# An unused 32-byte buffer beside the raw weights of a hybrid attention block: the ring of weight tiles moves down by 32 bytes in each partition

## The chip, the cores and the metric

The kernel runs on one core of one Trainium2 chip. The metric is device time in microseconds (us) of one execution. Three runs of the kernel before gave 836.05, 835.23 and 834.75 us, a median of 835.23 us.

## The reference

One layer of a decoder block on 512 tokens of width 1024. A projection of the normalised input feeds two token mixers, a chunked gated linear attention (GLA, 4 heads) and a sparse attention with a compressed, a selected and a window branch (NSA, 8 heads). Their gated sum goes through an output matrix and a normalisation, then a SwiGLU network of width 2816 follows. Cut to its frame:

```python
proj = rms_norm(x, norm_mix_pre) @ w_in
o_gla = gla_mixer(g_q, g_k, g_v, g_r, g_a, ...)
o_nsa = nsa_mixer(n_q, n_kc, n_vc, n_ks, n_vs, n_kw, n_vw, n_gate, ...)
mixed = sigmoid(merge_gla) * (o_gla @ w_proj_gla) + sigmoid(merge_nsa) * (o_nsa @ w_proj_nsa)
x = x + rms_norm(mixed @ w_out, norm_mix_post)
h = rms_norm(x, norm_ffn_pre)
f = (silu(h @ w_ffn_gate) * (h @ w_ffn_up)) @ w_ffn_down
x = x + rms_norm(f, norm_ffn_post)
```

All inputs and the output are float32.

## The kernel before

**Split products.** Every large product is made of three matmuls in the type fp32r. A weight tile is split into a high part and a low part (the rest), an activation tile likewise, and lines 243, 248 and 249 (function `three`) add high weight by high activation, high weight by low activation, and low weight by high activation. In the profile the first name behind the arrow is the moving operand, the second the stationary one that a weight load (PEld) brings into the array ahead of its matmul. Activations move and weights are stationary, except in line 569, the first projection (`w_tok`), where the weight tile moves (440 columns) and the activation is stationary.

**Stages.** From the start to about 66 us runs the first projection, with 440 columns a matmul. Up to 200 us follow products in a Strassen-like form (line 352 makes their sums), 256 columns a matmul, with some plain products of 512 columns between them. From 200 to 460 us most products move 512 columns: GLA's end, the compressed branch, from about 275 to 415 us the attention itself with transposes of the probabilities (line 1139), then the second part of `w_proj` (moving tiles `bh`, `bl`) and the first three products of `w_out`. From 460 to 705 us the matmuls move 256 columns again: the rest of `w_out` by halves, then the gate and up matrices of the SwiGLU network in the Strassen-like form. From 705 to 765 us the first part of `w_down` moves 512 columns, and the rest of `w_down`, again in that form, 256.

**Weights.** A raw weight tile (`wraw`, 128 by 1024, 4 KB in each partition, three buffers) is loaded by SyncE. ScalarE casts it to its high part `whi` (line 78 and others), VectorE subtracts to get the low part `wlo` (line 85 and others), or a DMA of GpSimd's queue adds the raw weights onto a negated high part (lines 82 and 1446). Two pairs of `whi` and `wlo` form the ring. Other weights stand in tiles of the left side: `d_two`, `c_two`, `w_uu`, `w_g3h`, `w_g3l`, `feq`, `eks`, `ekw`.

**Where tiles lie.** Class `Ring` holds two pools on the right side of the memory: `raws` for `wraw`, and below it the pool `ring`, which is closed and opened anew twice. `open(16)` puts a gap of 64 bytes above the four ring tiles, `open(0)` does not. So the ring lies at one of two places: from the opening at the kernel's start, and again from the fourth product of `w_out` on, it is at "place A"; from the nineteenth tile of the first stream of weights (about 210 us) to the third product of `w_out` (about 460 us) at "place B", 64 bytes lower. Below the ring, still on the right side, lie the attention's probabilities (`p`, `p0`, `mx`, `z`) and some merge gates (`tb`).

Addresses below are bytes within a partition, as the built program has them. In the kernel before, `wraw` begins at 217056 (32 mod 64, 96 mod 128); the ring at 200672 in place A (96 mod 128) and 200608 in place B (32 mod 128). The moving activations of lines 243 to 249 begin at 32 mod 128 nearly everywhere (`hT_hi` at 17824); the weights on the left side at 96 mod 128 (`d_two` at 161504).

**Order.** Each engine's list of instructions is laid down as the program is written, with `issue_after` and priorities as hints to the scheduler; semaphores tie the engines together. A function `restart` makes the next 256-column product issue its second matmul as two of 128 columns.

Of the kernel before, what the change touches and what calls it, by code (L numbers as in the profile page):

```python
# [8 lines left out]
F32 = mybir.dt.float32  # L9
# [27 lines left out]
class Stream:  # L37


    def __init__(self, tc, pool, ahead):  # L40
        self.tc, self.nc, self.pool, self.ahead, self.after = tc, tc.nc, pool, ahead, None
        self.src, self.done, self.pos, self.made = [], {}, 0, 0
        self.on_dma, self.place, self.limit, self.by_half, self.raws = set(), {}, None, set(), {}
        self.reset = None
# [59 lines left out]
class Ring:  # L104


    def __init__(self, ctx, tc):
        self.tc, self.pool, self.turn = tc, None, {}
        self.raws = ctx.enter_context(tc.tile_pool(name="raws", bufs=1, side="right"))
        ctx.callback(self.close)  # L110

    def close(self):
        if self.pool is not None:
            self.pool[1].__exit__(None, None, None)
        self.pool = None
# [1942 lines left out]
```

## Time and profile before

The profile shows one execution whose span, from the first to the last instruction, is 833.8 us. The page gives no total of that execution beside its span; the runs' median is 835.23 us, 1.4 us more than the span.

| engine | busy us | share of the span |
|---|---|---|
| PE (matmul) | 823.1 | 99% |
| PEld (weight load, beside PE) | 749.7 | 90% |
| DVE (VectorE) | 633.1 | 76% |
| ACT (ScalarE) | 526.2 | 63% |
| POOL (GpSimd) | 147.2 | 18% |

The matmul row is a union of overlapping spans: each matmul's span reaches past the start of the next, so a busy share of 99% says that the array was never without a matmul, not that it ran at its peak. The pace is read from the distance between starts (the timeline view) or from the count of matmuls in a stretch that is wholly busy. The granted TensorE clock is 1.00 in all stretches but the last.

### The profile page before, as it was taken

How to read it: one execution, taken by the hardware profiler on the slowest of the kernel's cores; microseconds unless marked ns; L12 is line 12 of the kernel's file. 1: busy time of each engine (PE TensorE's matmuls, PEld its weight loads, DVE VectorE, ACT ScalarE, POOL GpSimd, SP SyncE). 2: the span in 40 equal slices, each digit the busy share in tenths (PEclk: the TensorE clock that was granted, in tenths of full speed). 3: DMA queues.
4: the chain of work that ended last, by engine and by line, in shares of the span. 5: the costliest groups of instructions: out<-in, count | busy, mean ns of one | idle time of the engine just before them, and what ended most of it. 6: DMA issues, size and time to landing. Idle time of an engine off the chain costs nothing.

```text
span 833.8 us, 14626 instructions
## 1 busy us (share of the span) xinstructions
PE 823.1 (99%) x5553; PEld 749.7 (90%) x5553; DVE 633.1 (76%) x1198; ACT 526.2 (63%) x973; POOL 147.2 (18%) x176
## 2 busy tenths in 40 slices
PE   9999999999999999999999999999999999999996
PEld 8998899998788787888888999999999999889996
DVE  7765897883377888777666488998888778839985
ACT  6557767763454889887645587766665657535542
POOL 0101022230030000100000365111211110001354
PEclk9999999999999999999999999999999999999998
DMA  8333465762252454454228758789878883325333
GB/s 295 98 110 102 120 121 129 168 145 84 76 182 51 105 127 101 102 127 106 73 76 280 227 153 228 141 209 236 187 187 200 201 182 86 91 77 178 89 103 101
DMA packets 41239, 117.85 MB, mean 141 GB/s; under 512 B 4716, under 2 KB 7036, under 8 KB 41040
## 3 DMA queue, kind: packets, MB, share of 16 engines
q1 hardware_dynamic: 27952, 82.49, 31.9%
q0 software_dynamic: 12496, 33.88, 22.0%
q8 instruction: 43, 0.70, 0.3%
q10 hardware_dynamic: 720, 0.54, 0.2%
q14 instruction: 28, 0.23, 0.1%
HBM read 102.21 MB, written 4.19 MB: 128 GB/s over the span
## 4 chain that ended last, share of the span: by engine, by line
PE 88%; DVE 5%; ACT 4%; POOL 2%; issue 1%; POOLq 0%; DVEq 0%; ACTq 0%
PE ps_mm L243 13%; PE ps_mm L249 13%; PE ps_mm L248 13%; PE ps_sc L243 5%; PE ps_sc L249 5%; PE ps_sc L248 4%; PE ps_acc L248 3%; PE ps_acc L249 3%; PE ps_acc L243 3%; PE ps_tp L249 2%; PE ps_tp L243 2%; PE ps_tp L248 2%; PE ps_tp L569 2%; PE ps_sc L569 2%; PE ps_tp L1139 2%
## 5 line engine op out<-in xcount | busy, mean ns | idle before, releaser
L78 ACT CAST whi<-wraw 128x1024 fp32r<-128x1024 f32 (+2 forms) x62 | 60.2, 973 | 64.9 <-PE ps_mm L248 22.7
L243 PE MATMUL ps_mm<-hT_hi,whi 128*128 128x512 f32 (+1 forms) x260 | 100.1, 385 | 0.2 <-ACT whi L78 0.2
L249 PE MATMUL ps_mm<-hT_hi,wlo 128*128 128x512 f32 (+1 forms) x260 | 97.1, 374 | 0.0
L248 PE MATMUL ps_mm<-hT_lo,whi 128*128 128x512 f32 (+1 forms) x259 | 96.7, 374 | 0.0
L85 DVE TENSOR_TENSOR wlo<-wraw,whi 128x1024 fp32r<-128x1024 f32 (+2 forms) x47 | 51.4, 1096 | 27.0 <-ACT whi L78 26.9
L243 PEld LDWEIGHTS ps_mm<-hT_hi,whi 128*128 128x128 f32 x260 | 48.9, 188 | 10.2 <-ACT whi L78 0.9
L249 PEld LDWEIGHTS ps_mm<-hT_hi,wlo 128*128 128x128 f32 x260 | 48.8, 188 | 9.3 <-DVE wlo L85 0.3
L248 PEld LDWEIGHTS ps_mm<-hT_lo,whi 128*128 128x128 f32 x259 | 48.7, 188 | 7.5
L1462 ACT CAST d_two<-s 128x1024 fp32r<-128x1024 f32 x26 | 27.0, 1044 | 30.5 <-PE ps_mm L249 15.0
L274 DVE TENSOR_TENSOR pl<-ps_tp,ph 128x512 fp32r<-128x512 f32 (+1 forms) x64 | 31.2, 490 | 13.2 <-ACT ph L273 12.5
L1469 DVE TENSOR_TENSOR d_two<-s,d_two 128x1024 fp32r<-128x1024 f32 x25 | 30.6, 1223 | 11.2 <-ACT d_two L1462 10.9
L82 POOL DMA_DIRECT2D wlo<-wraw x15 | 12.8, 852 | 147.3 <-ACT wlo L81 71.3
L1101 ACT ACTIVATE p<-p,mx 128x512 f32<-128x512 f32 (+3 forms) x64 | 35.7, 559 | 4.6 <-DVE mx L1099 4.2
L1099 DVE CUSTOM_DVE_ANT_0 p<-ps_sc,causal 128x512 f32<-128x512 f32 (+3 forms) x64 | 30.0, 488 | 9.5 <-PE ps_sc L1093 8.6
L273 ACT CAST ph<-ps_tp 128x512 fp32r<-128x512 f32 (+1 forms) x64 | 26.6, 417 | 4.4 <-PE ps_tp L1139 3.4
L1838 POOL TENSOR_TENSOR y<-y,us 128x256 f32<-128x256 f32 x12 | 16.0, 1361 | 72.1 <-DVE us L1835 72.1
L1139 PE MATMUL ps_tp<-ident,p 128*128 128x128 f32 x160 | 27.7, 272 | 0.0
L1139 PEld LDWEIGHTS ps_tp<-ident,p 128*128 128x128 f32 x160 | 20.8, 140 | 7.2 <-ACT pc L1023 0.4
L1446 POOL DMA_DIRECT2D wlo<-in_w_gate x13 | 11.5, 887 | 76.8 <-ACT wlo L1444 76.7
L1462 ACT CAST c_two<-s 128x1024 fp32r<-128x1024 f32 x12 | 12.5, 1044 | 18.7 <-PE ps_acc L249 9.5
L243 PE MATMUL ps_mm<-hT_hi,d_two 128*128 128x256 f32 x80 | 22.3, 279 | 0.0
L249 PE MATMUL ps_mm<-hT_hi,d_two 128*128 128x256 f32 x80 | 22.3, 279 | 0.0
(841 smaller groups left out, 3214.6 us busy)
## 6 DMA issues: line engine op xcount, KB each, us to landing
wraw<-in_w_t SPq DMA_DIRECT2D x36, 512.0 KB, 3.9
wraw<-in_w_gate SPq DMA_DIRECT2D x21, 512.0 KB, 4.5
rw<-in_w_up SPq DMA_DIRECT2D x19, 512.0 KB, 8.3
wlo<-wraw POOLq DMA_DIRECT2D x15, 512.0 KB, 4.5
wlo<-in_w_gate POOLq DMA_DIRECT2D x13, 512.0 KB, 8.6
w_uu<-in_w_up POOLq DMA_DIRECT2D x19, 256.0 KB, 8.7
wraw<-in_w_tok SPq DMA_DIRECT2D x11, 440.0 KB, 3.4
wraw<-in_w_proj SPq DMA_DIRECT2D x8, 512.0 KB, 3.6
```

The source lines that it names most:

```text
L78: self.cast = self.nc.scalar.copy(hi[:, :cols], raw[:, :cols])
L85: self.nc.vector.tensor_tensor(out=lo[:, :cols], in0=raw[:, :cols], in1=hi[:, :cols].bitcast(F32), op=OP.subtract)
L243: pe.matmul(o, wh, xh, start=start, stop=False, skip_group_check=True)
L248: pe.matmul(o[:, c], wh, xl[:, c], start=False, stop=False, skip_group_check=True)
L249: return pe.matmul(o, wl, xh, start=False, stop=stop, skip_group_check=True)
L274: dve.tensor_tensor(out=lo, in0=src, in1=hi.bitcast(F32), op=OP.subtract)
L569: pe.matmul(o, x[:, k, t], y[:, w], start=(k == 0 and m == 0), stop=(k == KD - 1 and m == 2))
L1099: dve.tensor_tensor_reduce(out=o, in0=s, in1=causal[:, S - 128 * (i + 1):S], scale=-1.0, scalar=-NEG, op0=OP.add, op1=OP.min, accum_out=mx ...
L1101: act.activation(out=o, in_=o, func=AF.Exp, scale=-1.0, bias=mx[:, i:i + 1], accum_out=z[:, i:i + 1])
L1139: pe.transpose(tp[:, i * 128:(i + 1) * 128], p[:, OFF[i] + k * 128:OFF[i] + (k + 1) * 128] if i else p0, ident)
L1462: act.copy(hi, t)
L1469: dve.tensor_tensor(out=lo, in0=t, in1=hi.bitcast(F32), op=OP.subtract)
```

## The change

One tile of 128 partitions by 8 float32 (32 bytes in each partition) is asked for in the pool `raws`, before any raw weight tile. Nothing writes or reads it.

```diff
@@ -108,6 +108,7 @@
         self.tc, self.pool, self.turn = tc, None, {}
         self.raws = ctx.enter_context(tc.tile_pool(name="raws", bufs=1, side="right"))
         ctx.callback(self.close)
+        self.raws.tile([128, 8], F32, name="line")
 
     def close(self):
         if self.pool is not None:
```

No engine's list of instructions changes: all five hold the same rows in the same order with the same waits, apart from line numbers and buffer numbers. What changes is addresses. The words for the change are that raw weights and ring begin at 0 instead of 32 mod 64. In the built program the new room lies at the low end of `raws`, between it and the ring: the three `wraw` buffers keep their addresses (32 mod 64), and SyncE's instructions are the same byte for byte. All that lies below moves down by 32 bytes:

| tiles | before | after |
|---|---|---|
| `wraw` | 217056 (96 mod 128) | 217056 (96 mod 128) |
| ring, place A | 200672 (96 mod 128) | 200640 (64 mod 128) |
| ring, place B | 200608 (32 mod 128) | 200576 (0 mod 128) |
| `p`, three buffers | 32 mod 128 | 0 mod 128 |
| `p0`, `mx`, `z`, seven `tb` | 32 bytes lower each | |

Every tile on the left side stays.

## Prediction

> **What bounds the kernel now.** I read the page's busy shares and chain first.
>
> ```profile
> span 833.8 us, 14626 instructions
> PE 823.1 (99%) x5553; PEld 749.7 (90%) x5553; DVE 633.1 (76%) x1198; ACT 526.2 (63%) x973; POOL 147.2 (18%) x176
> PE 88%; DVE 5%; ACT 4%; POOL 2%; issue 1%; POOLq 0%; DVEq 0%; ACTq 0%
> ```
>
> TensorE carries 88% of the chain of waits. A change that moves no instruction can only act through how long instructions take, and only TensorE's pace reaches the end. So the second view is a table by stage of stretches in which TensorE is wholly busy (columns: stretch, its length, then busy time and count of PE, PEld, DVE, ACT and POOL, the granted clock, the DMAs):
>
> ```profile
> 446.00:459.00 13.00, 13.00 (x59) 10.74 (x59) 5.69 (x6) 7.66 (x10) 1.28 (x1) 1.00 0.96 355
> 542.00:554.00 12.00, 12.00 (x104) 12.00 (x104) 11.72 (x21) 6.58 (x10) 1.71 (x2) 1.00 0.76 209
> 570.00:700.00 130.00, 130.00 (x1149) 130.00 (x1149) 104.63 (x185) 80.11 (x124) 21.34 (x25) 1.00 0.80 185
> 720.00:740.00 20.00, 20.00 (x87) 16.14 (x86) 9.73 (x14) 7.19 (x11) 0.00 (x0) 1.00 0.30 81
> ```
>
> The clock is full in all four, and nobody waits. The third view is the timeline, for the distance between starts; first and last row of each stretch:
>
> ```profile
> 456.04 0.39 PE L249 MATMUL ps_mm<-hT_hi,wlo 128*128 128x512 f32 x1
> ...
> 459.44 0.39 PE L249 MATMUL ps_mm<-hT_hi,wlo 128*128 128x512 f32 x1
> ```
> ```profile
> 744.96 0.39 PE L243 MATMUL ps_acc<-hT_hi,whi 128*128 128x512 f32 x1
> ...
> 749.16 0.39 PE L243 MATMUL ps_tp<-hT_hi,whi 128*128 128x512 f32 x1
> ```
> ```profile
> 599.75 0.28 PE L243 MATMUL ps_sc<-x4h,w_g3h 128*128 128x256 f32 x1
> ...
> 603.49 0.28 PE L243 MATMUL ps_tp<-hT_hi,whi 128*128 128x256 f32 x1
> ```
> ```profile
> 546.89 0.28 PE L243 MATMUL ps_mm<-x,d_two 128*128 128x256 f32 x1
> ...
> 549.36 0.28 PE L249 MATMUL ps_tp<-hT_hi,d_two 128*128 128x256 f32 x1
> ```
>
> The first holds 15 steps in 3.40 us, 226.7 ns a matmul; the second 18 in 4.20 us, 233.3 ns. Both move 512 columns of the same `hT` against ring tiles, in the same form; what differs is where the ring lies: place B at 32 mod 128, place A at 96 mod 128, with the moving tile at 32 in both. The third holds 33 steps in 3.74 us, 113.3 ns for 256 columns; the fourth 21 in 2.47 us, 117.6 ns, with weights (96) and moving tiles (32) at the same places as in the third. So this core has two paces for each width, 3 to 4% apart. For 512 columns the offset between weights and moving tile goes with the pace (64 bytes apart is slow); for 256 columns, 64 bytes apart can be fast, and something in the history decides, since 542 to 554 us ran slowly and 570 to 700 us (1149 in 130 us) at the fast pace throughout. A stream of moving data and a stream of weights are read at the same time, and their relative phase matters: that is how I read it. It is argued from pace alone. One more case, moving tiles partly at 96, ring at 32:
>
> ```profile
> 420.95 0.39 PE L243 MATMUL ps_sc<-bh,whi 128*128 128x512 f32 x1
> ...
> 423.74 0.40 PE L243 MATMUL ps_sc<-bh,whi 128*128 128x512 f32 x1
> ```
>
> 12 steps in 2.79 us, 232.5 ns: in 8 of the 12 the moving tile (`bl`, and half of `bh`) stands 64 bytes off, and it is the slow pace again.
>
> No row of this trace has fp32r weights at 0 or 64 mod 128: that is what the change brings.
>
> **The change part by part.** Counts of matmuls are of the program; the ring is stationary in 336 of 512 columns at place A (14 products of 24), 744 of 512 at place B, and 1236 of 256 at place A; it moves in 288 of 440.
>
> *Ring at place B, 512 columns.* Of the 744, the attention's 360 and the 96 with `bh` already run between the paces or slowly (the row above, and in the attention the mean span is 392 where the fast stretch has 389 and the slow one 396):
>
> ```profile
> L248 PE MATMUL ps_mm<-hT_lo,whi 128*128 128x512 f32 x74 | 29.0, 392 | 0.0
> ```
> ```profile
> L243 PE MATMUL ps_mm<-hT_hi,whi 128*128 128x512 f32 x20 | 7.8, 389 | 0.0
> ```
> ```profile
> L243 PE MATMUL ps_sc<-hT_hi,whi 128*128 128x512 f32 x8 | 3.2, 396 | 0.0
> ```
>
> The other 288 are fast. Between nothing and the whole distance of 6.6 ns, that is 0 to +1.9 us; if all 744 were fast now, +4.9 us is the outer bound. The new place lies 32 bytes off the moving tile, midway between the two that are measured, so I take the middle, +3.3 ns: +1.0 us.
>
> *Ring at place A, 512 columns.* These 336 are slow now and can only keep that or gain: −2.2 us to 0, the middle −1.1 us.
>
> *Ring at place A, 256 columns.* Some of the 1236 stand in slow stretches; I take three quarters, 930, as fast now (an estimate from 570 to 700 us being fast and 542 to 554 us slow). 0 to +4.3 ns each; the middle 2.15 ns gives +2.0 us, the outer bound with all 1236 is +5.3 us.
>
> *The neighbours.* 2131 more matmuls of 256 columns take their weights from the left side, still at 96. Today all weights in the SwiGLU stage lie alike; afterwards ring tiles at 64 and others at 96 alternate, and each change of place shifts the phase. A slow stretch outlives the product that began it (the fourth timeline is slow on `d_two` alone). Bounds: the 145 us from 560 to 705 us, all fast now, slow down by 117.6/113.3, +5.5 us; or slow stretches elsewhere are cured, −1.5 us for the 40 us around 542 to 554 us. Loss has more room than gain here; I take a fifth of the loss, +1.1 us.
>
> *Ring as the moving operand, 440 columns.* A tile has two halves of 440 columns, 1760 bytes apart: one begins at 96 mod 128, the other at 64. The row that tells what 0 mod 64 does to a moving operand is therefore in the trace:
>
> ```profile
> 50.12 0.36 PE L569 MATMUL ps_tp<-whi,hu_hi 128*128 128x440 f32 x1
> 50.32 0.36 PE L569 MATMUL ps_tp<-whi,hu_lo 128*128 128x440 f32 x1
> 50.52 0.36 PE L569 MATMUL ps_tp<-wlo,hu_hi 128*128 128x440 f32 x1
> 50.72 0.36 PE L569 MATMUL ps_tp<-whi,hu_hi 128*128 128x440 f32 x1
> 50.92 0.36 PE L569 MATMUL ps_tp<-whi,hu_lo 128*128 128x440 f32 x1
> 51.12 0.36 PE L569 MATMUL ps_tp<-wlo,hu_hi 128*128 128x440 f32 x1
> 51.32 0.36 PE L569 MATMUL ps_sc<-whi,hu_hi 128*128 128x440 f32 x1
> ```
>
> Three from either half take 0.60 us. The halves now begin at 64 and 32. Zero, with a bound of 288 times 3% of 200 ns, ±1.7 us, by the two paces of the other widths.
>
> *Casts, subtractions and DMAs.* The cast onto the ring and the subtraction take what the same forms take on tiles elsewhere:
>
> ```profile
> L78 ACT CAST whi<-wraw 128x1024 fp32r<-128x1024 f32 x43 | 44.9, 1049 | 48.5 <-PE ps_mm L248 19.3 <-issue 10.3 <-PE ps_tp L248 5.4
> L1462 ACT CAST d_two<-s 128x1024 fp32r<-128x1024 f32 x26 | 27.0, 1044 | 30.5 <-PE ps_mm L249 15.0 <-PE ps_acc L249 13.9 <-DVE s L1478 1.4
> L85 DVE TENSOR_TENSOR wlo<-wraw,whi 128x1024 fp32r<-128x1024 f32 x28 | 34.1, 1222 | 18.9 <-ACT whi L78 18.8
> L1469 DVE TENSOR_TENSOR d_two<-s,d_two 128x1024 fp32r<-128x1024 f32 x25 | 30.6, 1223 | 11.2 <-ACT d_two L1462 10.9
> ```
>
> A few ns of a microsecond, and 99% of matmul time covers both engines; without that cover, 5 ns on each of some 110 such instructions would be 0.6 us. The raw weights do not move, so SyncE's loads cost nothing new, whatever the words for the change say. The DMAs that add onto `wlo` land as here:
>
> ```profile
> wlo<-wraw POOLq DMA_DIRECT2D x15, 512.0 KB, 4.5
> L249 PEld LDWEIGHTS ps_mm<-hT_hi,wlo 128*128 128x128 f32 x260 | 48.8, 188 | 9.3 <-DVE wlo L85 0.3
> ```
>
> The weight loads that use `wlo` name no DMA as what they waited for, so these too are covered; 10% on the landing would be 0.5 us inside slack.
>
> Sum: +1.0 − 1.1 + 2.0 + 1.1 = +3.0 us on the span of 833.8, 836.8; the runs lie about 1.4 us above it, **838.2 us**.
>
> [...]
>
> **The rivals.**
>
> *Nothing below 64 bytes matters* (chance 0.24). The pace would follow which 64-byte half of a 128-byte stretch a tile begins in, and 96 to 64, or 32 to 0, stay in their halves. For it: the 440-column halves at 96 and 64 are equal. Against: nothing measured, since 64 bytes is the smallest distance by which weights differ in this trace. Time 835.2, ±1 us. [...]
>
> *The ring lands in the good phase* (0.23). The 336 slow ones become fast, −2.2 us, and the slow 40 us are cured, −1.5: 831.5 us. For it: the two measured places each suit one width and fail the other, so neither is best for both. Against: most of the time is at the fast pace already.
>
> *Loads that begin on a 64-byte line are shorter* (0.06). 512 bytes from 32 mod 64 touch nine lines of 64 bytes, from 0 eight. If the 113.3 ns were set by the load and fell to the pace of the transposes, about 0.11 us each (four of them end 0.60 us after the first began, each spanning 272 ns),
>
> ```profile
> 321.98 0.60 PE L1139 MATMUL ps_tp<-ident,p 128*128 128x128 f32 x4
> L1139 PE MATMUL ps_tp<-ident,p 128*128 128x128 f32 x160 | 27.7, 272 | 0.0
> ```
>
> that is 3%: some −4 us on the 1236, −5 on the 744 and as much on the 336 with their way from 233.3: about 821 us. Against: a fast 512-column matmul has room for two loads and still takes twice 113.3.
> [...]
>
> *The phase slips for good* (0.10; the slow side at its full price). All ring products at the slow pace, +4.9 and +5.3, and half of the 2131 neighbours times 4.3 ns, +4.6, less 2.2: +12.6, 847.8 us. It decides from the point where a ring product leaves the next `d_two` product in the slow pace. For it: slow stretches last. Against: `restart` stands at the stages' beginnings.
>
> **How the numbers follow.** The moderate loss has 0.37, its own range 837 to 842. With 0.10 for the slip, slower holds 0.47; the first rival is same, 0.24; faster 0.23 + 0.06 = 0.29. Beyond 0.2%, 1.7 us, a measurement of this kernel tells a change from none. Range: 829 to 845, which leaves out the shorter loads and the full slip.
>
> **What would show it.** In the new profile: the 512-column span of 389 near 446 to 459 us and 396 near 720 to 740 us, the 276 of 256 columns between 570 and 700 us and the count of 1149 there. Middle values, or both 276 and 281 mixed by product, bear me out; all four unchanged is the first rival; 389 at 720 us with 276 kept is the second; under 276 the third. I am wrong if the time moves while these rows stand, since then DMAs or ScalarE carry it.

## The result and the profile after

The changed kernel took 840.62 us (median of four runs, 840.41 to 841.55) against 835.63 us for the kernel before beside it (834.75 to 836.05). The ratio is 1.0065, with a 95% interval of 1.0053 to 1.0077: slower by 5.0 us, on the side and within the range of the forecast, which had a loss of 3.0 us.

The first view is the page of the kernel after: the span, the engines' busy times, and the shares of the chain of waits.

```profile
span 838.7 us, 14626 instructions
...
PE 828.8 (99%) x5553; PEld 754.8 (90%) x5553; DVE 633.5 (76%) x1198; ACT 526.1 (63%) x973; POOL 146.2 (17%) x176
...
PE 93%; ACT 3%; DVE 2%; issue 1%; POOL 0%; POOLq 0%; ACTq 0%
```

The span grew by 4.9 us. TensorE's busy time grew by 5.7 us, VectorE's by 0.4, and ScalarE's and GpSimd's shrank a little. So the time is in TensorE's pace, as a change without a moved instruction suggests. The second view is the table by stage that the prediction used, of the kernel after (stretch, its length, busy time and count of PE, PEld, DVE, ACT, POOL, granted clock, DMA share, GB/s):

```profile
446.00:459.00 13.00, 13.00 (x57) 10.45 (x57) 6.89 (x8) 6.18 (x9) 0.98 (x1) 1.00 0.91 320
542.00:554.00 12.00, 12.00 (x105) 11.86 (x104) 12.00 (x22) 7.47 (x11) 1.70 (x2) 1.00 0.76 212
570.00:700.00 130.00, 130.00 (x1138) 130.00 (x1137) 103.90 (x184) 78.27 (x121) 21.99 (x26) 1.00 0.80 187
720.00:740.00 20.00, 20.00 (x88) 16.13 (x87) 12.43 (x20) 8.72 (x16) 0.00 (x0) 1.00 0.34 102
```

The granted clock is 1.00 in all four, as before. Between 570 and 700 us 1138 matmuls begin where 1149 did, and between 446 and 459 us 57 where 59 did. Where the time came in can be read by taking the same matmul (the n-th in the program; their names agree throughout) in both traces and comparing its start. The table cuts the program at times of the kernel before and gives the growth of each piece; the first pace is before, the second after.

| piece (us, before) | what runs | growth, us | pace, ns |
|---|---|---|---|
| 0 to 66 | 440 columns, ring moves | −0.28 | about 200 both |
| 66 to 200 | 256 and 512 columns, place A | +1.12 | mixed |
| 200 to 460 | 512 columns, place B | +1.66 | 226.7, 233.3 (446 to 459) |
| 460 to 560 | 256 columns, place A | +0.05 | mixed |
| 560 to 705 | 256 columns, place A | +1.53 | 113.3, 114.5 (570 to 700) |
| 705 to 752 | 512 columns, place A | +0.04 | 233.3, 233.3 |
| 752 to 827 | 256 columns, place A | +0.66 | mixed |

The first two pieces carry a scatter between executions. In the run with place B alone (below), every address used before about 210 us is that of the kernel before, and yet these pieces differ by −0.32 and +0.65 us.

Two timelines of the kernel after show these paces by starts. In the stretch that was fast before, near 446 us, first and last row (59 steps in 13.76 us, 233.2 ns, where 226.7 was):

```profile
446.06 0.39 PE L244 MATMUL ps_mm<-hT_hi,whi 128*128 128x512 f32 x1
...
459.82 0.40 PE L250 MATMUL ps_mm<-hT_hi,wlo 128*128 128x512 f32 x1
```

And in the SwiGLU network, where weights of the left side (`d_two` and others) and of the ring (`whi`, `wlo`) alternate:

```profile
599.83 0.28 PE L250 MATMUL ps_mm<-hT_hi,d_two 128*128 128x256 f32 x1
...
605.95 0.28 PE L250 MATMUL ps_mm<-x,d_two 128*128 128x256 f32 x1
606.07 0.28 PE L244 MATMUL ps_tp<-hT_hi,whi 128*128 128x256 f32 x1
...
607.37 0.28 PE L250 MATMUL ps_tp<-hT_hi,wlo 128*128 128x256 f32 x1
607.49 0.28 PE L244 MATMUL ps_tp<-hT_hi,d_two 128*128 128x256 f32 x1
...
611.46 0.28 PE L250 MATMUL ps_acc<-hT_hi,d_two 128*128 128x256 f32 x1
```

The 54 steps with left weights ahead of 605.95 take 6.12 us, 113.3 ns each, unchanged. The ring's 12 products then take 11 steps of 118.2 ns, and the 35 steps behind them with left weights 113.4 ns again. Over the whole piece from 560 to 705 us, 987 distances that lie wholly among left weights average 113.4 ns, those among ring tiles 118.1, and the two at the borders on the ring's side (the first step between ring tiles, and the step from the last ring tile) 122.5 and 123.0. So the loss stays with the ring's own products.

### The profile page after: what moved, and what is told of

It reads as the page before. It is cut to its first block, busy times and chain, and to the rows that moved or that the text cites. A ratio compares the mean times of both kernels' runs of the same rounds, so it can differ in the third digit from the quotient of the medians.

```text
span 838.7 us, 14626 instructions
## 1 busy us (share of the span) xinstructions
PE 828.8 (99%) x5553; PEld 754.8 (90%) x5553; DVE 633.5 (76%) x1198; ACT 526.1 (63%) x973; POOL 146.2 (17%) x176
## 4 chain that ended last, share of the span: by engine, by line
PE 93%; ACT 3%; DVE 2%; issue 1%; POOL 0%; POOLq 0%; ACTq 0%
PE ps_mm L244 14%; PE ps_mm L250 14%; PE ps_mm L249 14%; PE ps_sc L244 5%; PE ps_sc L250 5%; PE ps_sc L249 5%; PE ps_acc L250 3%; PE ps_acc L244 3%; PE ps_acc L249 3%; PE ps_tp L250 3%; PE ps_tp L244 3%; PE ps_tp L249 3%; PE ps_tp L570 2%; PE ps_sc L570 2%; PE ps_tp L1140 2%; PE ps_acc L1155 1%
## 5 line engine op out<-in xcount | busy, mean ns | idle before, releaser
L1463 ACT CAST d_two<-s 128x1024 fp32r<-128x1024 f32 x26 | 27.1, 1044 | 31.3 <-PE ps_mm L250 15.4
L1463 ACT CAST c_two<-s 128x1024 fp32r<-128x1024 f32 x12 | 12.5, 1044 | 18.9 <-PE ps_acc L250 9.7
```

The source lines that it names most:

```text
L1463: act.copy(hi, t)
```

## The experiments

The theory on trial, called **the relative offset**: TensorE's pace goes with where the weights begin minus where the moving tile begins, counted modulo some power of two. The picture behind it, that the two reads disturb each other, was the author's guess; what a trace shows is that weight loads run beside the matmuls (in the kernel before PEld, like PE, is busy 130.00 of the 130.00 us from 570 to 700). The rivals: **the absolute place** (a tile that begins on a line of 32 or 64 bytes is read faster or slower by itself), and **the raw weights** (their place, too, costs something). Nearly all moving tiles begin at 160 mod 256 (`hT_hi` at 17824), so the offsets of the ring, mod 256, are: place A 64 before and 32 after, place B 0 before and 224 after; the left weights stand at 64 in both. "Ratio" below is time over the time of the kernel before on the same chip, with its 95% interval.

### Bursts at 32 pairs of places

A kernel that runs only bursts of 24 matmuls: four moving tiles, begun at 0, 160, 64 and 224 mod 256 (`movA` to `movD`), and eight weight tiles at 0, 144, 32, 176, 64, 208, 96 and 240 (`wgtA` to `wgtH`); first 512 columns, then twice 256.

```diff
-    (the reference's work)
+    for n in (512, 256):
+        for m in mov:
+            for w in wts:
+                last = burst(m, w, n)
+    for m in mov[::-1]:
+        for w in wts[::-1]:
+            last = burst(m, w, 256)
```

> A kernel of bursts of 24 matmuls alone, without the block's computation: every moving tile at 0, 32, 64 or 96 mod 128 (names movA to movD) with every weight tile at 0, 16, 32 ... 112 mod 128 (wgtA to wgtH), for 512 columns, then 256, then 256 in the reverse order. Theory R (the offset of the weights from the moving tile decides): for 512 columns the spans are 389 ns only where weights minus moving is 0 mod 128, and about 393 to 396 at all others; for 256 columns 276 ns only where it is 64, and 279 to 281 elsewhere. The pattern then lies on a diagonal of the 4 by 8 table. Theory S (weights that begin at 0 mod 64 are slow by themselves): 276 and 389 for wgtC and wgtG with every moving tile, more for wgtA and wgtE with every one.

The groups of matmuls of this kernel by line and shape (busy, mean ns of one span; roughly, a span of 389 goes with a pace of 226.7 ns, 392 with 230.0, 395 to 396 with 233.3, 397 with 234.6):

```profile
L66 PE MATMUL ps<-movB,wgtA 128*128 128x512 f32 x24 | 5.8, 397 | 0.0
L66 PE MATMUL ps<-movA,wgtG 128*128 128x512 f32 x24 | 5.8, 397 | 0.0
...
L66 PE MATMUL ps<-movA,wgtD 128*128 128x512 f32 x24 | 5.7, 392 | 0.0
L66 PE MATMUL ps<-movC,wgtH 128*128 128x512 f32 x24 | 5.7, 392 | 0.0
```

The first two rows have tiles at wholly different places (160 and 0; 0 and 96) and the same offset of 96: 234.6 ns both. The last two (0 and 176; 64 and 240) share the offset 176: 230.0 ns both. In these bursts the pace goes with the difference, and modulo 128 is not enough: 64 had 233.3 ns and 192 had 228.8, 48 had 233.3 and 176 had 230.0. A tile's own place does not set the pace: `movA` met paces from 226.7 to 234.6 ns. Where several pairs share an offset they agree to 0.3 ns, except at 128, 208 and 240, where they differ by up to 1.6 ns. The expectation had counted modulo 128 and fails there: the shortest spans, 389 to 391 ns, stand at offsets 0, 144 and 240, while 128 has 395; and for 256 columns 276 ns came at 64 in one of the two passes only, and not at 192.

### Left side and ring both moved: everything at 0 mod 64

```diff
     base = ctx.enter_context(tc.tile_pool(name="base", bufs=1, reuse_waits="tile"))
+    base.tile([128, 8], F32, name="pad")
...
         ctx.callback(self.close)
+        self.raws.tile([128, 24], F32, name="line")
```

The moving tiles and left weights move up by 32 bytes, the ring down by 96: the ring now begins at 0 mod 64 as in the changed kernel, but its offset to the moving tiles changes by 128 in place of 32.

> All tiles of the left side 32 bytes up, the ring 96 bytes down: moving tiles at 64 mod 128, left weights at 0, ring at 0 in place A and 64 in place B. Every offset between weights and moving tiles is that of the kernel before, but nearly all tiles begin at 0 mod 64. Theory R: 835.6 us as before, ratio 0.998 to 1.002, 276 ns on 256 columns and 389 on 512 at 446 to 459 us. Theory S: all weights slow, 3400 matmuls of 256 columns by 4 ns and 744 of 512 by 6, about 850 us.

835.9 us, ratio 1.0012 (1.0002 to 1.0021). The stage table of this kernel:

```profile
446.00:459.00 13.00, 13.00 (x57) 10.55 (x56) 5.80 (x7) 6.95 (x9) 1.29 (x1) 1.00 0.93 348
570.00:700.00 130.00, 130.00 (x1149) 130.00 (x1149) 105.08 (x186) 79.38 (x122) 21.34 (x25) 1.00 0.79 186
720.00:740.00 20.00, 20.00 (x89) 16.40 (x88) 10.51 (x15) 7.97 (x12) 0.00 (x0) 1.00 0.29 82
```

The 1149 matmuls of 113.3 ns are back, although every ring tile begins on a line of 64 bytes. The absolute place falls as the cause of the loss. The time is near the kernel before, but not for the reason expected: the paces of 512 columns did not stay. Near 446 us they went from 226.7 to 232.4 ns (57 matmuls, not 59; 1.23 us more from 200 to 460 us), and from 720 to 740 us from 233.3 to 228.9 ns (0.83 us less from 705 to 752 us). At an offset shifted by 128 the pace was another here, as in the bursts (233.3 ns at 64, 228.8 at 192).

### The left side alone

```diff
     base = ctx.enter_context(tc.tile_pool(name="base", bufs=1, reuse_waits="tile"))
+    base.tile([128, 8], F32, name="pad")
```

The ring keeps its addresses; all on the left side, moving tiles and weights, moves up by 32 bytes. The ring's offset changes as by the change, and the left weights keep theirs.

> All tiles of the left side 32 bytes up, the ring as in the kernel before (96 in place A, 32 in place B), moving tiles at 64, left weights at 0. Theory R: ring products have the odd offset (32 one way or the other) and are as slow as after the change, products with left weights as fast as before; about 840.6 us, 256-column spans of 279 or more for whi and 276 for d_two. Theory S: the ring fast (276), the left weights slow (2131 matmuls by about 4 ns), about 843 us, with 276 for whi and 280 for d_two.

840.72 us, ratio 1.0067 (1.0052 to 1.0082). The stage table:

```profile
446.00:459.00 13.00, 13.00 (x57) 10.44 (x57) 6.92 (x8) 6.62 (x10) 0.95 (x1) 1.00 0.88 323
570.00:700.00 130.00, 130.00 (x1138) 130.00 (x1137) 103.92 (x184) 78.28 (x121) 22.11 (x26) 1.00 0.80 187
```

The same counts, 57 and 1138, as in the kernel after, and the growth of the pieces from 560 to 705 us (+1.53), 705 to 752 (+0.04) and 752 to 790 us (+1.27) is the same to 0.01 us. A kernel in which no ring tile moved has the change's loss (840.72 us beside 840.62): here the difference counts and not the ring's own place.

### The raw weights moved too

```diff
     def __init__(self, ctx, tc):
         self.tc, self.pool, self.turn = tc, None, {}
+        ctx.enter_context(tc.tile_pool(name="end", bufs=1, side="right")).tile([128, 8], F32, name="line")
         self.raws = ctx.enter_context(tc.tile_pool(name="raws", bufs=1, side="right"))
```

This is what the words for the change say: 32 bytes at the very end of the memory, so that raw weights as well as the ring begin at 0 mod 64.

> What the words of the change say: the 32 bytes lie at the very end of the memory, so that the raw weights begin at 64 mod 128 (0 mod 64) too, and the ring lies where the change puts it. Theories R and S: the raw weights' place costs and brings nothing, 840.6 us as with the change, ratio to it within 0.2%. A third theory, that loads or casts pay for raw weights and ring lying differently mod 64: back towards 835.6 us, with the cast of 1049 ns or the subtraction of 1222 ns shorter.

840.72 us, ratio 1.0068 (1.0053 to 1.0083), beside 1.0065 for the change. Where the raw weights lie costs nothing that can be measured here.

### Place A alone, place B alone

```diff
+        self.raws.tile([128, 8], F32, name="line")
-            self.pool.open(16)
+            self.pool.open(8)
```

The second line holds place B where it was, so that only place A moves. In the other kernel place B moves, and with it what lies below it there (the attention's probabilities among them):

```diff
-            self.pool.open(16)
+            self.pool.open(24)
```

> The ring 32 bytes lower in place A alone (64 mod 128), in place B as before the change (32). Theory R: the 512-column products from 214 to 460 us are as fast as before, the 256-column ones with ring weights as slow as with the change; of the 5.0 us about 3.3 remain, 838.4 us (837.6 to 839.2). If the loss came from one place alone: 835.1 or 840.1.

> The ring 32 bytes lower in place B alone (0 mod 128), in place A as before the change (96). Theory R: only the 512-column products from 214 to 460 us pay, 1.7 us: 836.8 us (836.0 to 837.6), and onlyA and onlyB together make up the whole loss. If the two places disturb each other the sum of both losses is far from 5.0 us.

Place A alone: 838.97 us, ratio 1.0046 (1.0031 to 1.0061). Place B alone: 836.84 us, ratio 1.0018 (1.0008 to 1.0027). Both lie in the ranges expected. The two losses, 0.46% and 0.18%, make 0.64%, beside the 0.65% of the change. From the stage table with place A alone, and then with place B alone:

```profile
446.00:459.00 13.00, 13.00 (x58) 10.71 (x58) 6.17 (x7) 6.46 (x9) 1.28 (x1) 1.00 0.95 335
...
570.00:700.00 130.00, 130.00 (x1138) 130.00 (x1137) 103.91 (x183) 78.29 (x121) 21.43 (x26) 1.00 0.79 187
```
```profile
570.00:700.00 130.00, 130.00 (x1149) 130.00 (x1148) 105.21 (x184) 79.67 (x124) 21.60 (x26) 1.00 0.80 187
```

The 256-column loss belongs to place A (1138 against 1149), and the 512-column pace near 446 us to place B: by starts 227.2 ns with A alone moved, 233.3 with B alone. A stretch of 13 us may hold one matmul more or less by where its borders fall; the starts decide. With place B alone the 57 steps between these two rows take 13.30 us:

```profile
446.14 0.39 PE L249 MATMUL ps_mm<-hT_hi,wlo 128*128 128x512 f32 x1
...
459.44 0.40 PE L249 MATMUL ps_mm<-hT_hi,wlo 128*128 128x512 f32 x1
```

### A buffer of 128 bytes in place of 32

```diff
+        self.raws.tile([128, 32], F32, name="line")
```

This brings place A to offset 192 and place B to 128; modulo 128 both offsets are the old ones.

> The unused buffer at 128 instead of 32 bytes, so that the ring lies at 96 (place A) and 32 (place B) mod 128 as before, but is shifted by half of 256. Theory R128 (the offset counts mod 128): nothing changes, 835.1 us. Theory R256 (it counts mod 256, which the bursts show: the same offset mod 128 gave 233.3 and 226.7 ns): place A then stands 192 off the moving tile, 256 columns at about 117.5 ns, 512 at 229 (fast gain of 1.4 us); place B 128 off, 512 columns at 232.5: about 838.6 us (837 to 840).

835.91 us, ratio 1.0006 (0.9996 to 1.0015). The 512-column products followed the bursts, which say modulo 256: between 720 and 750 us 228.9 ns where 233.3 was (−0.83 us from 705 to 752 us), near 446 us 233.3 where 226.7 was (+1.3 us from 200 to 460 us). The expectation for 256 columns failed, and with it the 838.6 us: at offset 192 they kept 113.3 ns from 570 to 700 us, 1150 matmuls in the 130 us.

```profile
570.00:700.00 130.00, 130.00 (x1150) 130.00 (x1149) 105.08 (x186) 79.39 (x122) 21.34 (x25) 1.00 0.79 186
720.00:740.00 20.00, 20.00 (x89) 16.38 (x89) 10.69 (x16) 8.01 (x12) 0.00 (x0) 1.00 0.29 83
```

That made a finer measurement necessary.

### Bursts at 32 offsets

One moving tile at 160 mod 256 as in the kernel, weight tiles at every multiple of 8 bytes from it (`wgtaa` at 0, `wgtba` at 32, `wgtca` at 64, `wgtdd` at 120, `wgtga` at 192, `wgtha` at 224). After 512 columns come three passes with 256 columns: upwards, downwards, and upwards with the second matmul of each burst cut in two halves, as `restart` does it in the kernel.

```diff
-    (the reference's work)
+    for w in wts:
+        burst(m, w, 512)
+    for w in wts:
+        burst(m, w, 256)
+    for w in wts[::-1]:
+        burst(m, w, 256)
+    for w in wts:
+        last = burst(m, w, 256, 3, True)
```

> Bursts alone, without the block: one moving tile at 160 mod 256, as hT in the block, and weights at 32 places 8 bytes apart round 256, named aa to hd: for 512 columns, for 256 columns in both orders, and for 256 columns with the second matmul cut into two of 128. Theory R256: the pace is a function of the offset alone: 512 columns 226.7 to 228 ns at 0, 144 and 240, 229 to 230 at 176 and 192, 232 to 233.5 at the others; 256 columns 113.3 ns at 64 in at least one of the passes, 116.5 to 120 elsewhere. Theory A (absolute places count too): values that differ from the first bursts at the same offset by over 1 ns. If the cut sets the phase: 113.3 at 64 in the last pass.

512 columns, the first burst with each tile (groups by line and shape):

```profile
L70 PE MATMUL ps<-mov,wgtba 128*128 128x512 f32 x24 | 5.8, 396 | 0.0
...
L70 PE MATMUL ps<-mov,wgtca 128*128 128x512 f32 x24 | 5.8, 396 | 0.0
...
L70 PE MATMUL ps<-mov,wgtha 128*128 128x512 f32 x24 | 5.8, 395 | 0.0
...
L70 PE MATMUL ps<-mov,wgtga 128*128 128x512 f32 x24 | 5.7, 391 | 0.0
...
L70 PE MATMUL ps<-mov,wgtdd 128*128 128x512 f32 x24 | 5.6, 389 | 0.0
```

The offsets of this case, with paces by starts over the last 12 steps of a burst, beside what the kernels showed where their ring stood at that offset:

| offset mod 256 | where | 512 columns: burst, kernel | 256 columns: bursts (three passes), kernel |
|---|---|---|---|
| 0 | B before | 226.7, 226.7 | 120.0, 120.0, 120.0; 120.0 (A with 64 bytes, below) |
| 32 | A after | 233.3, 233.3 | 118.3, 118.8, 118.8; 118.1 |
| 64 | A before, left weights | 233.3, 233.3 | 113.3, 113.3, 117.8; 113.3 and 117.6 |
| 128 | B with 128 bytes | 232.6, 233.3 | 120.0, 118.2, 118.8; none |
| 192 | A with 128 bytes | 228.9, 228.9 | 117.8, 117.8, 113.3; 113.3 (570 to 700 us) |
| 224 | B after | 233.3, 233.3 | 116.7, 117.8, 116.7; none |

For 512 columns the bursts give the kernel's pace to within 1 ns, and so the direction of each term of the change: B from 0 to 224 is the whole way from 226.7 to 233.3, A from 64 to 32 is no way at all. For 256 columns at offset 32, the change's place A, no burst on record was fast: all ten lie between 118.0 and 118.8 ns. The curve is not smooth, and several offsets missed the expected bands: of all 32 offsets only 0 and 120 reach 226.7, 8 bytes from 0 already cost 3.9 ns (230.6), and 16, 32 and 40 to 72 stand at 233.3. For 256 columns the fast pace appears at 64, 88, 168 and 192 alone, and there not in every pass: two paces exist at these offsets (113.3 and 117.8 ns at 64 and at 192), so the addresses alone do not decide; that what ran ahead decides is the author's guess, and no run shows it. Nor does the cut decide: at 64 the pass with it is the slow one (117.8 ns, 113.3 without), at 192 the fast one (113.3, 117.8 without). Two windows of this kernel's groups, the first pass and then the third, show it for offset 64:

```profile
L70 PE MATMUL ps<-mov,wgtca 128*128 128x256 f32 x24 | 2.9, 276 | 0.0
```
```profile
L70 PE MATMUL ps<-mov,wgtca 128*128 128x256 f32 x23 | 3.1, 284 | 0.0
```

### A buffer of 64 bytes

```diff
+        self.raws.tile([128, 16], F32, name="line")
```

Place A comes to offset 0, place B to 192. Every tile is again at 32 mod 64.

> An unused buffer of 64 bytes: place A comes to offset 0 to the moving tile, place B to 192, both mod 256. If the offset decides, the 512-column products at place A run at 226.7 ns between 720 and 750 us (336 times 6.6 ns, -2.2 us), those at place B at 228.9 between 446 and 459 us (+0.6 to +1.3 us), and the 256-column products at 118 to 120 ns, as the bursts at offset 0 ran (1236 times 3 to 5 ns in the kernel, +3.7 to +6 us): 837.5 to 840 us, about 838.5. If a tile's own place, a line of 64 or 128 bytes, decides, all ring tiles lie as good or as bad as before at 32 mod 64: 835.2 us with no change of pace.

844.2 us, ratio 1.0111 (1.0095 to 1.0126). Both 512-column paces came as the bursts say: by starts 228.9 ns near 446 us, 226.7 between 720 and 750 us. The groups of the last stretch, 720 to 740 us, and the stage table:

```profile
L244 PE MATMUL ps_sc<-hT_hi,whi 128*128 128x512 f32 x16 | 6.2, 389 | 0.0
```
```profile
570.00:700.00 130.00, 130.00 (x1102) 130.00 (x1101) 101.22 (x179) 75.54 (x117) 21.29 (x25) 1.00 0.79 185
```

But 256 columns lost more than expected, +6.2 us from 560 to 705 us alone, and the groups by line of 570 to 700 us tell why:

```profile
L250 PE MATMUL ps_acc<-hT_hi,d_two 128*128 128x256 f32 x36 | 10.1, 281 | 0.0
...
L244 PE MATMUL ps_acc<-x5h,w_uu 128*128 128x256 f32 x28 | 7.9, 281 | 0.0
```

These products take left weights, at offset 64 as ever, and they run slowly: 117.8 ns on average over 987 distances, 4.4 us more, beside 120.0 ns among the ring tiles. It is the only run on record in which left weights are slow in this stage: beside ring products at offset 0 they take 117.8 ns, beside those of the change (offset 32) 113.4. Why is open.

### Which of the two reads matters

Bursts at six offsets (`wgta` to `wgtf`: 0, 32, 64, 128, 192, 224), with half and a quarter of the weight columns, with one weight column read 128 times, with one moving column read 512 times, and with both.

```diff
+                if wide:
+                    y = w[:, k * 128:k * 128 + 1].to_broadcast([128, 128])
+                if still:
+                    x = m[:, k * S:k * S + 1].to_broadcast([128, n])
```

> Only bursts of matmuls run, the reference's work is left out. At offsets 0, 32, 64, 128, 192 and 224: products of 512 columns with all 128 weight columns, with 64, with 32, with one weight column read 128 times (step 0), with one moving column read 512 times (step 0), with both, and products of 256 columns with all weights. If the pace is lost where the two reads meet, the 6.6 ns between offset 0 and offset 32 shrink with the number of weight columns, to about 3 ns at 64 and 2 ns at 32, and vanish where one of the reads does not advance. If each product pays a set-up that depends on the two addresses, the 6.6 ns stay with 64 and 32 columns. The full bursts of 512 columns are 226.7, 233.3, 233.3, 232.4, 228.9 and 233.3 ns, as before.

The groups by line of this kernel (`psfull` all weights, `pswide` one weight column, `psstill` one moving column):

```profile
L71 PE MATMUL psfull<-mov,wgtb 128*128 128x512 f32 x24 | 5.8, 395 | 0.0
...
L71 PE MATMUL pswide<-mov,wgta 128*128 128x512 f32 x24 | 5.7, 394 | 0.0
L71 PE MATMUL pswide<-mov,wgtb 128*128 128x512 f32 x24 | 5.7, 394 | 0.0
...
L71 PE MATMUL psfull<-mov,wgta 128*128 128x512 f32 x24 | 5.6, 389 | 0.0
...
L71 PE MATMUL psstill<-mov,wgta 128*128 128x512 f32 x24 | 5.3, 379 | 0.0
L71 PE MATMUL psstill<-mov,wgtb 128*128 128x512 f32 x24 | 5.3, 379 | 0.0
```

With all weights the paces are those of before: 226.7, 233.3, 233.3, 231.7, 228.9, 233.3 ns. Where the weight read stays on one column, all six offsets run at 231.7; where the moving read stays on one column, all six at 215.8, and so with both still. So in these bursts the offset made a difference only where both operands advance, and with all weights a moving operand that advances took 11 to 18 ns a matmul more (226.7 to 233.3) than one that stands (215.8). The proportion to the weight columns did not come: with 64 columns 230.0 against 231.7 ns (offsets 0 and 32), with 32 columns 231.7 against 240.0. A set-up per product that depends on the two first addresses does not fit, since `pswide` and `psstill` begin at the same pairs of addresses as `psfull` and show no difference (231.7 and 215.8 ns at all six). The simple form of the theory, that fewer columns meet less often, fails too; why the pace goes with the offset is open.

### Place A by 128 bytes, place B as before

```diff
-    wts.open(0)
+    wts.open(32)
```

At both openings of place A: offset 192 there, 0 at place B. That combines paces found above (at 192 228.9 ns for 512 columns and 113.3 for 256, at 0 226.7 for 512) without moving the left side or the raw weights.

> The ring's first tiles are shifted by 128 bytes at place A only (offset to the moving tile 192 mod 256, as in the run with a buffer of 128 bytes); place B stays at offset 0. The offset alone decides: place A's 512-column products run at 228.9 ns instead of 233.3 between 720 and 750 us, its 256-column products at 113.3 ns as before, place B's 512-column products at 226.7 ns between 446 and 459 us. From the run with 128 bytes, the loss of its stages between 200 and 460 us, 1.3 us, falls away and the gain after 705 us stays: about 833.8 us, a ratio near 0.998. The rival, that history in a stage decides as much as the offset: between 835 and 836 us, with the 720 us stretch or the 570 us stretch not at these paces.

834.77 us against 835.29, ratio 0.9995 (0.9986 to 1.0004): no difference that can be told, and 1.0 us above what was expected. The stage table:

```profile
446.00:459.00 13.00, 13.00 (x59) 10.77 (x58) 5.84 (x7) 7.53 (x10) 1.28 (x1) 1.00 0.99 360
...
570.00:700.00 130.00, 130.00 (x1150) 130.00 (x1149) 104.60 (x185) 79.72 (x124) 21.28 (x25) 1.00 0.80 185
720.00:740.00 20.00, 20.00 (x89) 16.43 (x88) 10.08 (x15) 7.53 (x12) 0.00 (x0) 1.00 0.31 86
```

In the three stretches the paces came as expected (226.8, 113.3 and 228.9 ns by starts), and the trace shows the gain, −0.83 us from 705 to 752 us; at 827 us the kernel is 0.76 us ahead. Between 110 and 200 us 0.48 us was lost. That piece alone proves little, since with place B alone it lost 0.42 us with no address moved there. But of the 431 products of 256 columns with ring weights between 66 and 210 us, only 24 are fast (the next start follows in at most 114 ns), where 269 are in the kernel before and 151 with place B alone. With the same moving tile `hT`, 10 of 107 are fast there, and 41 of 42 behind 790 us. So at the one offset 192 the pace differs by stage: the rival of the expectation, history in a stage, has a part. The offset can be chosen, as the 228.9 ns between 720 and 750 us show, but no gain in the kernel's time was shown with it.

## Why the prediction was right, and where not

The direction was right, and so was the reading that TensorE's pace goes with the place of the weights relative to the moving tile (840.62 us with the ring moved, 840.72 with the left side moved in its stead); that a phase between two streams lies behind it, and that each change of place shifts it, no run shows. "Two paces for each width" was too coarse: the bursts at 32 offsets run from 226.7 to 234.3 ns for 512 columns. The table gives what each group of matmuls added: for each matmul the distance to the next start, after less before, summed over the group from the two profiles. With place B alone, where place A and the left side kept their addresses, the sums for place A's 256 columns, the left weights and the 440 columns are +0.2, +0.4 and −0.2 us in place of nothing, so a figure here is good to about 0.4 us.

| group | forecast, us | measured, us |
|---|---|---|
| ring at place B, 512 columns (744) | +1.0 | +2.0 |
| ring at place A, 512 columns (336) | −1.1 | 0.0 |
| ring at place A, 256 columns (1236) | +2.0 | +3.6 |
| left weights, 256 columns (2131) | +1.1 | −0.1 |
| ring moving, 440 columns (288) | 0 | −0.2 |
| all other matmuls | 0 | −0.6 |
| sum (rows rounded) | +3.0 | +4.8 |

The step that failed is taking the middle between two measured places. Below, a product of 512 columns is called fast when the next start follows in at most 228 ns, one of 256 when in at most 114 ns.

- *Ring at place B, 512 columns.* The offset went from 0 to 224, where the pace is the slow one entirely. Of the 288 products that the forecast called fast, 209 were fast before and 3 after; together the 288 added 1.2 us. The forecast's 1.0 was near this only because not all of the 288 were fast. A second step failed here: the attention's 360 and the 96 with `bh` were put at nothing as slow already, but 117 and 25 of them were fast before (32 and 1 after), and they added 0.6 and 0.2 us.
- *Ring at place A, 512 columns.* 64 and 32 both stand at 233.3 ns, so the bound at nothing was reached and not the middle.
- *Ring at place A, 256 columns.* The estimate that three quarters, 930, were fast was good: 893 were fast before, and 5 after. The price was not: 3.6 us on 893 is 4.0 ns each, nearly the whole 4.3 and not half of it. In the SwiGLU network 210 distances among ring tiles went from 113.4 to 118.1 ns, and the two steps at the borders of each group are 9 to 10 ns above the fast pace.
- *The neighbours.* 987 distances between 560 and 705 us went from 113.3 to 113.4 ns: products with left weights came back within one step (about 116 ns, then 113.4). The fear was right in kind: with 64 bytes it happened, at 4.4 us in the same piece. Why it did not at offset 32 is open, as said above.
- *440 columns, casts, DMAs.* Forecast nothing, and what the first piece shows (−0.28 us) is within the scatter (−0.32 with place B alone). The transposes that take the moved `p` as weights kept their mean span of 272 ns. The casts and subtractions kept their durations (1049 and 1044 ns, 1222 ns), and the GpSimd DMA onto `wlo` its landing time (4.5 us), as the kernel after shows in its groups and its list of DMA issues:

```profile
L78 ACT CAST whi<-wraw 128x1024 fp32r<-128x1024 f32 x43 | 45.0, 1049 | 49.1 <-PE ps_mm L249 20.1 <-issue 10.5 <-PE ps_tp L249 5.4
L85 DVE TENSOR_TENSOR wlo<-wraw,whi 128x1024 fp32r<-128x1024 f32 x28 | 34.1, 1222 | 19.4 <-ACT whi L78 19.3
...
L1463 ACT CAST d_two<-s 128x1024 fp32r<-128x1024 f32 x26 | 27.1, 1044 | 31.3 <-PE ps_mm L250 15.4 <-PE ps_acc L250 14.3 <-DVE s L1479 1.3
```
```profile
wlo<-wraw POOLq DMA_DIRECT2D x15, 512.0 KB, 4.5
```

So two losses were under-sized (by 1.0 and 1.6 us) and a gain of 1.1 us did not come; a loss of 1.1 us that did not come and 0.8 us in the last two groups set off about half of that. That the sum came so near is in part luck. It was 1.9 us short on the span (838.7 against 836.8). Of the 2.4 us between 838.2 and 840.62 the rest lies around the span: each run on record takes 1.7 to 1.9 us more than its own span, and the forecast's 1.4 set a median beside the span of another execution.

Of the signs named in advance, the one for 256 columns came in its mixed form: 276 to 277 ns for most groups with left weights between 570 and 700 us, 280 to 284 for those with ring tiles. The middle values for 512 columns did not come: the stretch near 446 us is at the slow pace entirely.

The rivals. *Nothing below 64 bytes matters*: fallen, a 32-byte shift of the ring costs 0.65%, one of the left side 0.67%, and in bursts 8 bytes change the pace (226.7 ns at offset 0, 230.6 at 8). *The ring lands in the good phase*: fallen for 32 bytes, though offsets with the fast pace exist (0 for 512 columns, 226.7 ns; 64 and 192, each in some stages, for 256, 113.3 ns), and none tried in the kernel is the best for both (256 columns take 120.0 ns at 0, 512 columns 233.3 at 64 and 228.9 at 192). *Loads that begin on a 64-byte line are shorter*: fallen, with everything at 0 mod 64 the pace of 256 columns is 113.3 ns and not less. *The phase slips for good*: not at offset 32 (left weights at 113.4 ns); the run with 64 bytes (117.8 ns) is this rival in part.

## What to carry to other kernels

Where TensorE is busy throughout and matmul pace differs between stretches that look alike in a trace, compare the starting addresses of weights and moving tiles, as a difference modulo 256: here that was 3% of a matmul's time for 512 fp32r columns (226.7 to 233.3 ns), and up to 6% for 256 (113.3 to 120.0). Here a buffer that nobody touches moved all that lay below it, and the time grew by 0.65% with 32 bytes and by 1.1% with 64, so an edit elsewhere may do the same; before crediting an edit with such a difference, see whether the paces of untouched stages changed. Don't interpolate between two offsets, since the measured curve has jumps (512 columns: 226.7 ns at 0 and 120, 230.6 at 8, 233.3 at 16): a kernel of bursts over the offsets gave the kernel's 512-column paces to within 1 ns. For 256 columns it gave them only where the offset has a single pace.

## What was unexpected in the hardware

- Offsets 128 bytes apart gave different paces, 226.7 ns at 0 and 232.6 at 128 for 512 columns (modulo 256 the bursts agree, but for the third point), and the grain is fine: 8 gives 230.6, 16 gives 233.3 and 120 gives 226.7 again.
- Products of 256 columns have two paces at the same offset, 113.3 and 117.8 ns at 64 and at 192. In the kernel with 64 bytes, products whose own addresses hadn't changed went from 113.3 to 117.8 ns throughout a stage of 145 us. What chooses between the two isn't settled. Neither addresses nor order fix it: before about 210 us the run with place B alone has both as the kernel before has them, and of its 431 ring products of 256 columns there 151 were fast, against 269.
- Most pairs of places in the first bursts have the pace of the same difference in the finer ones to within 1.6 ns, but offset 144 had 226.7 ns there (twice) and 233.3 here; so 512 columns may have two paces at an offset as well, or the places themselves count there; no run separates the two. No stage of the kernel stands at that offset.
- With all weights, a moving operand that stays on one column runs 11 to 18 ns faster a matmul than one that advances (215.8 ns against 226.7 to 233.3 over the six offsets). Loading fewer weight columns shifts the paces without a simple order: with 64 columns 228.3 to 232.6 ns over the six offsets, with 32 columns 230.6 to 240.0, never as fast as the 226.7 of all 128 at offset 0.
